# Two mixers of a transformer block: convolution taps moved to VectorE, reciprocal roots to one GpSimd power, attention operands filled to 128 rows

## The chip, the cores and the metric

The kernel runs on one core of one Trainium2 chip. The metric is the time that the device takes for one execution, in microseconds (us), and smaller is better. A core has five engines that run side by side, each with an instruction queue of its own that it works through in order: TensorE (PE in the rows; PEld is its weight load), VectorE (DVE), ScalarE (ACT), GpSimd (POOL) and SyncE (SP), which here issues the transfers.

## What is computed

Two transformer blocks, one behind the other, on 512 tokens of 1024 channels, all in float32. The first (a differential attention layer and a Fourier layer with their feed-forwards) is touched by the change only in the norm of its queries and keys. The second has two layers, each a mixer and a convolutional feed-forward. The mixer runs four branches on quarter-width groups of the projected stream and joins them:

```python
proj = h @ w_in[l]
a_in, b_q, b_k, b_v, c_in, d_cq, d_ckv, d_kr = jnp.split(proj, SPLIT_POINTS, axis=-1)
# (a) gated convolution over 31 tokens, then layer norm and silu
a = a_in[..., :GROUP_W] * jax.nn.sigmoid(a_in[..., GROUP_W:])
a = depthwise_conv(a, conv_a_w[l], conv_a_b[l])
o_a = jax.nn.silu(layer_norm(a, ln_a_g[l], ln_a_b[l]))
# (b) grouped-query attention: rms norm of q and k, rotation, softmax(q k) v, heads of 64
# (c) spatial gating: gelu, layer norm of one half, a 128x128 product over tokens, times the other half
# (d) latent attention: rms norms, two small projections, rotation, heads of 64 + 32 channels
mix = jnp.concatenate([o_a, o_b, o_c, o_d], axis=-1) @ w_out[l]
h = layer_norm(DEEPNORM_ALPHA * h + mix, ln_mix_g[l], ln_mix_b[l])
```

## The kernel before

Activations lie feature-major, 128 channels on the partitions and 512 tokens along a row. Each large product is made of three passes over operands that are split in a high and a low part (`mm3`, lines 246 to 256: L250 low weights or activations first, L252 high with high, L254 the rest). `split` makes the parts: ScalarE copies the high part (L222), VectorE or GpSimd subtracts it to get the low part (L223). Weights arrive in three raw buffers, and their split parts live in four buffers each, so a unit of weights can be split only when the products that used an older one are done.

`mixer` is written as a list of 38 steps. Ahead of them stand: the projection of branch (b) with `head_rope` for each of four token tiles (rms norm, rotation), the constants of the attention operands, the projection of branch (a) into `ap` (padded by 15 columns at both ends), then `gate` for four token tiles (branch (c): gelu on ScalarE, mean and variance on VectorE, a reciprocal root, the scaling L1022, gain and shift L1023 and L1024, a split), each followed by `top` of the first head, two products `gelu_u`, and `shift` of the first head.

A step (h, t) works on head h of eight and key tile t of four. `top` (L1118, L1119) multiplies queries by keys and takes each query's maximum on VectorE; `shift` (L1125) turns the maxima into a row of the query operand, so that the score product subtracts them; `scores` (L1132 to L1134, exponential L1136) and `values` (L1142) follow; `sums` (L1151, L1153) and `leave` (L1163) divide and write the head's output three and five steps after its last. Maxima of head h + 1 are taken in the first two steps of head h. Steps 0 to 3 also carry `latent` (branch (d)'s down projection, two reciprocal roots at once, L1003 uses them), steps 4 and 5 the rest of branch (c), and steps 7 to 18 `mla_in` and `turn_mla`, which make the operands of the four latent heads, in tiles that `mla_tiles` takes at steps 7 and 14. Step 26 ends the convolution (`last`, `conv_out`). The output product begins behind the steps and takes the convolution's two chunks sixth and seventh of eight.

The convolution has 31 taps on each of two channel chunks. `conv_steps` gives nine of them to VectorE (L1253 and L1255, one instruction each, into `ya`) and 22 to GpSimd (a product L1259 into `cx` and an addition L1261 into `yb`, two instructions each); `conv_out` adds `yb` to `ya` (L1232). Its VectorE instructions may be placed only behind the last gate's scaling (`self.mark`); its GpSimd instructions have no such limit.

A reciprocal root is `rsqrt` (L285 to L291): twelve VectorE instructions on a few values per partition, a bit trick and three rounds of refinement. `head_rope` calls it through `rstd` (20 times in the first attention, four times per mixer), `latent` and `gate` directly (four times each per mixer). The other norms use `pow_half` (L314), one GpSimd instruction.

The framework decides the order of instructions on each engine when the program is built, from the order in which they are written, their dependencies and estimated durations; `issue_after(x)` keeps what is written inside it behind x on x's engine. On the chip that order is fixed.

Of the kernel before, what the change touches and what calls it, by code (L numbers as in the profile page):

```python
# [28 lines left out]
# columns of the packed feature-major vectors  # L29
# [19 lines left out]
# columns of the packed row vectors  # L49
# [15 lines left out]
class Seg:  # L65
    """a run of tokens: columns lo..lo+w of x(k) for feature chunk k, columns off..off+w of the split activations"""
# [11 lines left out]
class Part:  # L78
    """tokens that share a PSUM bank in a product, and the segments that norms take one after the other"""
# [5 lines left out]
class Ps:  # L85
    """PSUM pool with a number of buffers per tag"""
# [8 lines left out]
class RmsMod:  # L95
    """rms norm with gain, scale and shift, into the split activations H"""
# [10 lines left out]
    def ahead(self, xn, seg, r=None):  # L107
        """normed values without gain and shift"""
        pr = self.net.row_bcast(self.sums(seg) if r is None else r)
        for k in range(KD):  # L110
            self.net.V.tensor_tensor(xn[:, k, seg.cols()], seg(k), pr, ALU.mult)
        self.early[seg.off] = xn
# [31 lines left out]
class LayerNorm:  # L144
    """layer norm of the stream in place, and its split in H (or each chunk handed to out)"""
# [27 lines left out]
class Net:  # L173
# [16 lines left out]
    def phase(self, ctx, name, tbufs, reuse="tile"):  # L190
        """open the scratch pool of a phase"""
# [22 lines left out]
    # ---- weights: raw float32 in, split into two float32r parts that add up to it  # L214
# [21 lines left out]
    def units(self, src, ks, n):  # L236
        """ks blocks of n columns, as many per unit as fit"""
# [8 lines left out]
    def mm3(self, outs, lhs, start, stop):  # L246
        """outs: list of (psum, rhs hi, rhs lo); lhs: (hi, lo)"""
# [13 lines left out]
    def later(self, steps, work):  # L261
        """have work done behind that many steps of products"""
        self.pending.append((self.steps + steps, work))

    def product(self, outs, lhs):
        """outs: list of (psum, k -> rhs hi, k -> rhs lo); lhs: list over k of (hi, lo)"""
# [4 lines left out]
    def constant(self, dst, rows, one, eng=None):  # L271
        """fill rows of a float32r tile [p, m, n] with 0 or 1"""
        (eng or self.G).memset(dst[rows].bitcast(F32), float(one))

    # ---- small vector arithmetic
    def rstd(self, dst, src, scale, eps):
# [3 lines left out]
        self.rsqrt(dst, v)  # L280

    def rsqrt(self, dst, v):
        V, w = self.V, v.shape[1]
        hv, t = self.small(w), self.small(w)
        V.tensor_scalar(t.bitcast(I32), v.bitcast(I32), 1, None, ALU.logical_shift_right)  # L285
        V.tensor_scalar(dst.bitcast(I32), t.bitcast(I32), -1, 0x5F3759DF, ALU.mult, ALU.add)
        V.tensor_scalar(hv, v, -0.5, None, ALU.mult)
        for _ in range(3):
            V.tensor_tensor(t, dst, dst, ALU.mult)  # L289
            V.tensor_tensor(t, t, hv, ALU.mult)  # L290
            V.scalar_tensor_tensor(dst, t, 1.5, dst, ALU.add, ALU.mult)  # L291

    def bcast(self, dst, cols):
        """dst psum [128, 128*n]: row vector of cols[128 tok, n] on every partition"""
# [3 lines left out]
    def col_sums(self, dst, x):  # L298
        """dst psum [128 tok, n]: sums over the partitions of x [128, n*128 tok]"""
# [11 lines left out]
    def pow_half(self, dst, v):  # L311
        """dst = v ** -0.5 on GpSimd"""
# [17 lines left out]
    def row_ln(self, acc, accq, w, n):  # L330
        """rstd and mu*rstd per token, on every partition; sums over n channels"""
# [22 lines left out]
    # ---- setup  # L354
# [39 lines left out]
    # ---- the nine modulation vectors of a layer, for one or both conditions  # L394
# [47 lines left out]
    def fill(self, n):  # L442
        """advance the pending modulation vectors by n steps"""
# [16 lines left out]
    def norm_scale(self, l, i, msc):  # L460
        """g * (1 + scale) for norm i of layer l: [128, 8, 2]"""
# [7 lines left out]
    # ---- product that ends in the stream: weights stationary, one unit list per chunk of output features.  # L469
    # The last chunks go segment by segment, so that the norm of one segment runs beside the product of the next.  # L470
# [21 lines left out]
    # ---- gated feed-forward on the split activations H  # L492
# [79 lines left out]
    # ---- first block, layer 0: differential attention  # L572
    def head_rope(self, pt, G, out, tabs):
        """pt psum [128, G*64] -> out: rms norm over 64, gain and rotation folded in the tables"""
# [18 lines left out]
    def rotate(self, src, cosg, sing, o3, q):  # L593
        """src [128, G, 4q]; pairs are (0,q), (2q,3q) blocks; sing holds -sin first, +sin second"""
# [11 lines left out]
    def rope_tables(self, cos, sin, g, w, tiles, scale=1.0):  # L606
        """cos [128, 4, w], sin signed; g [128, w]: tables with the gain folded in"""
# [21 lines left out]
    def qkv(self, H, QT, KT, VV):  # L629
        """queries and keys normed, rotated, feature-major; values token-major; context tokens are tiles 4 and 5"""  # L630
# [52 lines left out]
    def diff_attention(self, QT, KT, VV, O, keep):  # L683
        """O[h]: split feature-major outputs of head h. p0 - lam*s0/s1*p1 stands for the attention; the factor 1/s0 of
        each query goes into the norm over the head's channels: 1/s0 / sqrt(ms/s0^2 + eps) = 1/sqrt(ms + eps*s0^2)."""
# [115 lines left out]
    # ---- first block, layer 1: Fourier mix on half spectra  # L801
# [74 lines left out]
    # ---- second block  # L876
    def proj_tm(self, us, n, H, tt):
        """token-major product of token tile tt"""
# [12 lines left out]
    def mixer(self, l, H, norm):  # L891
# [19 lines left out]
        # attention operands per pair of heads: queries and keys feature-major, one head per block, then a row that  # L911
        # takes minus the maximum of each query (ones on the side of the keys); values token-major with ones between
# [6 lines left out]
        def constants(q, k, vv, rows, zero):  # L919
# [50 lines left out]
        def step(n):  # L970
            for _ in range(n):
                with self.tc.issue_after(self.mark):
                    next(conv, None)
# [543 lines left out]
```

## Time and profile before

| | us |
|---|---|
| median of 3 timed runs (3626.2 to 3633.18) | 3630.28 |
| span of the profiled execution, first to last instruction | 3633.2 |
| TensorE busy | 3425.2 (94%) |
| TensorE weight loads busy | 2839.1 (78%) |
| VectorE busy | 2084.7 (57%) |
| ScalarE busy | 1267.5 (35%) |
| GpSimd busy | 517.0 (14%) |

The profile lists no other time for its own execution than the span, and the span is as long as the longest timed run. It is one execution, recorded by the hardware. "Busy" of TensorE is the time in which at least one product is under way; products overlap, so a busy TensorE need not run at full pace. The granted clock is the share of full speed at which TensorE is allowed to run: 0.5 is 1.2 GHz and 1.0 is 2.4 GHz, and a value between them is a mean over a stretch with both. Idle time before an instruction is put down to the instruction that ended last before it could start. `x16` is a count, `128x512 f32` a shape (partitions by columns).

### The profile page before, as it was taken

Reading aid. Unit: us, or ns where it says so; the run is one execution under the profiler, and the core shown is the slowest. Engines: PE = TensorE matmul, PEld = TensorE weight load, DVE = VectorE, ACT = ScalarE, POOL = GpSimd, SP = SyncE. Lnnn points to the kernel's source line nnn. Section 1 sums busy time; section 2 is a strip of 40 time slices with the busy share of each in tenths; the row PEclk is TensorE's granted clock in tenths of the full one; section 3 lists DMA queues with packets and bytes.
Section 4 is the critical chain, followed back from the end, with each engine's and each line's share of the span. In section 5 each row is a group of like instructions: output and inputs, shape, how many; then the busy total and the mean of one; then the engine's idle time right before and its main releaser. Section 6 shows DMA issues by size and latency. Waiting matters only on the chain.

```text
span 3633.2 us, 44413 instructions
## 1 busy us (share of the span) xinstructions
PE 3425.2 (94%) x17540; PEld 2839.1 (78%) x17540; DVE 2084.7 (57%) x3447; ACT 1267.5 (35%) x2180; POOL 517.0 (14%) x481
## 2 busy tenths in 40 slices
PE   7999999999999999999999999669999994999998
PEld 5888888777787778888888888557888873688887
DVE  6554355667664555333463336985744679666556
ACT  3211214336542224222452224235533441554333
POOL 1000001015410001000120003740100049020001
PEclk9999999999999999999999999879999996899999
DMA  6343352120045563333223333101333320023232
GB/s 222 122 141 112 101 161 72 50 70 1 24 154 160 181 195 123 99 95 97 74 99 93 93 98 91 41 21 47 93 95 97 93 80 14 18 70 110 90 102 64
DMA packets 99449, 341.80 MB, mean 94 GB/s; under 512 B 10916, under 2 KB 14116, under 8 KB 98984
## 3 DMA queue, kind: packets, MB, share of 16 engines
q1 hardware_dynamic: 99240, 338.96, 30.0%
q8 instruction: 138, 2.26, 0.3%
q14 instruction: 71, 0.58, 0.1%
HBM read 336.82 MB, written 2.10 MB: 93 GB/s over the span
## 4 chain that ended last, share of the span: by engine, by line
PE 35%; issue 6%; DVE 5%; POOL 4%; ACT 1%; ACTq 0%; DVEq 0%; POOLq 0%
PE mm L250 12%; PE mm L254 11%; PE mm L252 11%; POOL yb L1261 2%; POOL cx L1259 1%; DVE wl L223 1%; DVE ya L1255 0%; DVE s L290 0%; DVE s L291 0%; DVE s L289 0%; DVE t L164 0%; DVE t L165 0%; ACT H L222 0%; POOL s L314 0%; ACT X L166 0%
## 5 line engine op out<-in xcount | busy, mean ns | idle before, releaser
L222 ACT ACTIVATE wh<-wr 128x1024 fp32r<-128x1024 f32 (+4 forms) x505 | 510.9, 1014 | 1364.3 <-PE mm L252 894.2
L250 PE MATMUL mm<-H,wh 128*128 128x512 f32 (+1 forms) x2592 | 968.0, 374 | 11.6 <-DVE nm L1119 5.8
L254 PE MATMUL mm<-H,wl 128*128 128x512 f32 (+1 forms) x2592 | 963.0, 372 | 1.5 <-DVE wl L223 1.4
L252 PE MATMUL mm<-H,wh 128*128 128x512 f32 (+1 forms) x2592 | 964.2, 372 | 0.0
L223 DVE TENSOR_TENSOR wl<-wr,wh 128x1024 fp32r<-128x1024 f32 (+4 forms) x505 | 602.5, 1194 | 445.5 <-ACT wh L222 435.7
L250 PEld LDWEIGHTS mm<-H,wh 128*128 128x128 f32 x2592 | 494.6, 191 | 103.5 <-DVE nm L1119 6.5
L254 PEld LDWEIGHTS mm<-H,wl 128*128 128x128 f32 x2592 | 493.9, 191 | 85.8 <-DVE wl L223 2.3
L252 PEld LDWEIGHTS mm<-H,wh 128*128 128x128 f32 x2592 | 495.0, 191 | 83.5 <-issue 0.5
L254 PE MATMUL mm<-ah,wl 128*128 128x512 f32 (+1 forms) x1216 | 445.9, 367 | 0.0
L252 PE MATMUL mm<-ah,wh 128*128 128x512 f32 (+1 forms) x1216 | 443.8, 365 | 0.0
L250 PE MATMUL mm<-al,wh 128*128 128x512 f32 (+1 forms) x1216 | 443.1, 365 | 0.0
L252 PEld LDWEIGHTS mm<-ah,wh 128*128 128x128 f32 x1216 | 228.3, 188 | 42.4
L250 PEld LDWEIGHTS mm<-al,wh 128*128 128x128 f32 x1216 | 228.3, 188 | 42.3 <-issue 1.2
L254 PEld LDWEIGHTS mm<-ah,wl 128*128 128x128 f32 x1216 | 228.7, 188 | 39.5
L419 DVE SCALAR_TENSOR_TENSOR macc<-wr,SC,macc 128x1024 f32<-128x1024 f32 x133 | 168.3, 1281 | 94.3 <-DMA wr<-w_mod 93.7
L568 DVE SCALAR_TENSOR_TENSOR X<-mm,ng,X 128x512 f32<-128x512 f32 (+1 forms) x120 | 81.3, 678 | 244.8 <-PE mm L254 244.7
L314 POOL TENSOR_TENSOR s<-s,mhalf 128x2 f32<-128x2 f32 (+1 forms) x26 | 21.0, 806 | 1355.5 <-ACT s L321 816.4
L250 PE MATMUL mm<-wl,H 128*128 128x512 f32 (+2 forms) x480 | 180.7, 378 | 33.7 <-DVE wl L223 30.4
L528 DVE TENSOR_TENSOR act<-act,mm 128x512 f32<-128x512 f32 x88 | 60.3, 686 | 240.0 <-PE mm L254 239.8
L254 PE MATMUL mm<-wh,H 128*128 128x512 f32 (+2 forms) x480 | 176.7, 370 | 0.3
L252 PE MATMUL mm<-wh,H 128*128 128x512 f32 (+2 forms) x480 | 176.4, 368 | 0.0
L156 POOL TENSOR_TENSOR cx<-X 128x512 f32<-128x512 f32 x5 | 9.3, 1851 | 1005.7 <-DVE X L1267 638.2
(348 smaller groups left out, 4921.9 us busy)
## 6 DMA issues: line engine op xcount, KB each, us to landing
wr<-gu SPq DMA_DIRECT2D x176, 512.0 KB, 3.5
wr<-w_mod SPq DMA_DIRECT2D x136, 512.0 KB, 4.2
wr<-up SPq DMA_DIRECT2D x88, 512.0 KB, 3.5
wr<-dn SPq DMA_DIRECT2D x48, 448.0 KB, 3.4
wr<-down SPq DMA_DIRECT2D x32, 448.0 KB, 3.3
wr<-qkv SPq DMA_DIRECT2D x24, 512.0 KB, 4.3
wr<-dn SPq DMA_DIRECT2D x24, 512.0 KB, 3.6
wr<-w_out SPq DMA_DIRECT2D x16, 512.0 KB, 3.5
```

Source lines behind the costliest of these rows:

```text
L156: (net.G if k < KD - 1 else net.V).tensor_tensor(self.acc[:, sl], self.acc[:, sl] if k > 1 else seg(0), seg(k), ALU.add)
L222: self.S.activation(hi, src, AF.Copy)
L223: (eng or self.V).tensor_tensor(lo, src, hi.bitcast(F32), ALU.subtract)
L250: self.PE.matmul(pt, lh, rl, start=start, stop=False)
L252: self.PE.matmul(pt, lh, rh, start=False, stop=False)
L254: last = self.PE.matmul(pt, ll, rh, start=False, stop=stop)
L314: G.tensor_tensor(dst, v, self.mhalf.to_broadcast([P, w]), ALU.pow)
L419: self.V.scalar_tensor_tensor(acc[c], raw, s, acc[c], ALU.mult, ALU.add)
L528: self.V.tensor_tensor(to, to, pu, ALU.mult)
L568: self.V.scalar_tensor_tensor(s(d), pt, gate[0][:, d, s.cond:s.cond + 1], s(d), ALU.mult, ALU.add)
L1259: G.tensor_tensor(x, ap[:, j, t2:t2 + T], wt(t2).to_broadcast([P, T]), ALU.mult)
L1261: G.tensor_tensor(yb[:, j], yb[:, j], x, ALU.add)
```

## The change

The change has four parts. First, `rsqrt` is gone: `rstd`, `latent` and `gate` call `pow_half`, one GpSimd instruction, instead. Second, all 31 taps are VectorE instructions into `ya`; `yb`, `cx` in the convolution and the two additions in `conv_out` are gone. The taps are handed out two (one per chunk) in each of steps 1 to 25 and four in every fourth step, behind the latest `top` on VectorE (`self.mark2`) instead of the last gate. Third, the attention operands get zeros in all rows behind their channels (64 to 127 for branch (b), 96 to 127 for branch (d), which had none) and the products take all 128 rows instead of 96 or 97. Fourth, the constants of the latent heads' tiles are filled by GpSimd instead of VectorE. Comments are removed as well. The core of the diff:

```diff
     def rstd(self, dst, src, scale, eps):
         w = src.shape[1]
         v = self.small(w)
         self.V.tensor_scalar(v, src, scale, eps, ALU.mult, ALU.add)
-        self.rsqrt(dst, v)
-
-    def rsqrt(self, dst, v):
...
+        self.pow_half(dst, v)
...
-        def constants(q, k, vv, rows, zero):
+        def constants(q, k, vv, row):
             for i in range(2):
-                for x in (k, *q) if zero else ():
-                    self.constant(x[i], rows, 0)
-            eng = G if zero else V
-            eng.memset(vv[:, :, 1], 1.0)
-            self.constant(k[0], slice(rows.start, rows.start + 1), 1, eng)
+                for x in (k, *q):
+                    self.constant(x[i], slice(row, P), 0)
+            G.memset(vv[:, :, 1], 1.0)
+            self.constant(k[0], slice(row, row + 1), 1)
...
-        constants(q, k, vv, slice(64, 96), True)
+        constants(q, k, vv, 64)
...
         def step(n):
             for _ in range(n):
-                with self.tc.issue_after(self.mark):
+                with self.tc.issue_after(self.mark2):
                     next(conv, None)
...
-            self.rsqrt(r, ss)
+            self.pow_half(r, ss)
...
-            self.rsqrt(r, mv[:, 1:2])
-            self.mark = V.tensor_scalar(t, t, mv[:, 0:1], r, ALU.subtract, ALU.mult).ins
+            self.pow_half(r, mv[:, 1:2])
+            V.tensor_scalar(t, t, mv[:, 0:1], r, ALU.subtract, ALU.mult)
...
-            constants(*mla[i], slice(96, 97), False)
+            constants(*mla[i], 96)
...
-            PE.matmul(st, d["q"][0][:96, qi * P:qi * P + P], d["k"][0][:96], start=True, stop=True)
+            PE.matmul(st, d["q"][0][:, qi * P:qi * P + P], d["k"][0], start=True, stop=True)
...
-            PE.matmul(st, kl[:96, ks], qh[:96], start=True, stop=False)
-            PE.matmul(st, kh[:K, ks], qh[:K], start=False, stop=False)
-            PE.matmul(st, kh[:96, ks], ql[:96], start=False, stop=True)
+            PE.matmul(st, kl[:, ks], qh, start=True, stop=False)
+            PE.matmul(st, kh[:, ks], qh, start=False, stop=False)
+            PE.matmul(st, kh[:, ks], ql, start=False, stop=True)
...
-                 26: [lambda: step(99), last]}
+                 26: [last]}
...
-            if i > 5:
-                step(1)
+            if 0 < i < 26:
+                step(2 if i % 4 == 3 else 1)
...
     def conv_out(self, ya, O, v):
         V, S = self.V, self.S
-        for j in range(2):
-            V.tensor_tensor(ya[:, j], ya[:, j], self.yb[:, j], ALU.add)
...
     def conv_steps(self, ap, ya, w, b):
-        """31 taps, the first on VectorE and the others on GpSimd"""
-        V, G = self.V, self.G
-        NV = 9
-        yb = self.tile([P, 2, T], "yb")
-        for t in range(max(NV, 31 - NV)):
+
+        for t in range(31):
             for j in range(2):
-                wt = lambda t: w[:, 31 * j + t:31 * j + t + 1]
+                wt = w[:, 31 * j + t:31 * j + t + 1]
                 if t == 0:
-                    V.tensor_scalar(ya[:, j], ap[:, j, :T], wt(0), b[:, j:j + 1], ALU.mult, ALU.add)
-                elif t < NV:
-                    V.scalar_tensor_tensor(ya[:, j], ap[:, j, t:t + T], wt(t), ya[:, j], ALU.mult, ALU.add)
-                t2 = NV + t
-                if t2 < 31:
-                    x = self.tile([P, T], "cx", 2) if t else yb[:, j]
-                    G.tensor_tensor(x, ap[:, j, t2:t2 + T], wt(t2).to_broadcast([P, T]), ALU.mult)
-                    if t:
-                        G.tensor_tensor(yb[:, j], yb[:, j], x, ALU.add)
+                    self.V.tensor_scalar(ya[:, j], ap[:, j, :T], wt, b[:, j:j + 1], ALU.mult, ALU.add)
+                else:
+                    self.V.scalar_tensor_tensor(ya[:, j], ap[:, j, t:t + T], wt, ya[:, j], ALU.mult, ALU.add)
             yield
-        self.yb = yb
```

## Rows read from the trace of the kernel before

**Rows 1.** The page's busy tenths in 40 equal slices of the span, two of its lines.

```profile
PE   7999999999999999999999999669999994999998
PEclk9999999999999999999999999879999996899999
```

**Rows 2.** Stretches: length, each engine's busy us (instructions), granted clock, DMA share, GB/s.

```profile
2300.00:2404.00 104.00, 48.73 (x217) 40.59 (x216) 102.37 (x125) 12.86 (x30) 103.84 (x80) 0.71 0.05 15
2404.00:2440.00 36.00, 32.27 (x137) 24.58 (x137) 25.91 (x106) 17.21 (x52) 0.00 (x0) 0.81 0.13 44
2440.00:2507.00 67.00, 66.86 (x326) 46.74 (x324) 38.97 (x91) 41.78 (x88) 1.94 (x3) 0.97 0.08 25
2990.00:3093.00 103.00, 46.08 (x212) 39.17 (x211) 101.61 (x123) 12.86 (x30) 102.57 (x79) 0.71 0.05 13
```

**Rows 3.** What TensorE waited for, 2284 to 2404: total us, times, longest us.

```profile
PE tr L983 <- ACT t L1003: 16.2, 1, 16.2
PE mm L250 <- DVE wl L223: 14.8, 2, 12.0
PE tr L296 <- DVE nm L1119: 13.8, 2, 13.2
```

**Rows 4.** VectorE by line and shape, 2300 to 2404: count, busy us, mean ns, idle.

```profile
L1255 DVE SCALAR_TENSOR_TENSOR ya<-ap,vec,ya 128x512 f32<-128x512 f32 x16 | 21.9, 1388 | 0.0
L290 DVE TENSOR_TENSOR s<-s,s 128x1 f32<-128x1 f32 x12 | 11.8, 993 | 0.2
L1022 DVE TENSOR_SCALAR t<-t,s,s 128x256 f32<-128x256 f32 x4 | 4.8, 1212 | 0.0
L1119 DVE TENSOR_REDUCE nm<-mm 128x1 f32<-128x512 f32 x7 | 4.6, 672 | 0.0
L287 DVE TENSOR_SCALAR s<-s 128x1 f32<-128x1 f32 x3 | 0.4, 137 | 0.0
```

**Rows 5.** The same view, 2405 to 2497.

```profile
L1119 DVE TENSOR_REDUCE nm<-mm 128x1 f32<-128x512 f32 x24 | 15.8, 681 | 3.7 <-PE mm L1118 3.5
L290 DVE TENSOR_TENSOR s<-s,s 128x2 f32<-128x2 f32 x7 | 1.1, 154 | 0.1
L1234 DVE TENSOR_TENSOR t<-ya 128x512 f32<-128x512 f32 x1 | 0.7, 692 | 0.0
```

**Rows 6.** TensorE by line and shape, 2300 to 2404.

```profile
L250 PE MATMUL mm<-wl,H 128*128 128x352 f32 x25 | 10.9, 436 | 14.8 <-DVE wl L223 14.8
L250 PE MATMUL mm<-H,wh 128*128 128x512 f32 x16 | 7.8, 490 | 3.0 <-DVE nm L1119 3.0
L254 PE MATMUL mm<-wh,H 128*128 128x256 f32 x21 | 5.9, 283 | 0.0
```

**Rows 7.** TensorE in order of time: start, us, what; beside a full granted clock.

```profile
2457.01 0.28 PE L254 MATMUL mm<-wh,ck 128*128 128x256 f32 x1
2457.12 0.39 PE L1132 MATMUL mm<-q,k 96*128 96x512 f32 x1
2457.36 0.39 PE L1133 MATMUL mm<-q,k 96*128 96x512 f32 x1
2457.58 0.39 PE L1134 MATMUL mm<-q,k 96*128 96x512 f32 x1
```

**Rows 8.** GpSimd by line and shape, whole span.

```profile
L1261 POOL TENSOR_TENSOR yb<-yb,cx 128x512 f32<-128x512 f32 x84 | 120.0, 1447 | 0.3
L314 POOL TENSOR_TENSOR s<-s,mhalf 128x2 f32<-128x2 f32 x24 | 18.9, 788 | 1355.3 <-ACT s L321 816.4 <-PE mm L254 538.1
L273 POOL MEMSET q<- 32x1024 f32 x8 | 7.4, 951 | 0.1
```

**Rows 9.** GpSimd in order of time, one row.

```profile
2263.05 0.95 POOL L273 MEMSET q<- 32x1024 f32 x1
```

**Rows 10.** VectorE in order of time, two rows.

```profile
2263.24 1.23 DVE L223 TENSOR_TENSOR wl<-wr,wh 128x1024 fp32r<-128x1024 f32 x1 [0.20 <-ACT wh L222]
...
2488.32 1.28 DVE L1232 TENSOR_TENSOR ya<-ya,yb 128x512 f32<-128x512 f32 x2
```

More of the change, by code (lines that the diff above doesn't have):

```diff
@@ L279, in rstd @@
         self.V.tensor_scalar(v, src, scale, eps, ALU.mult, ALU.add)
-        self.rsqrt(dst, v)
-    def rsqrt(self, dst, v):
[L283 to L291, printed above, removed]
+        self.pow_half(dst, v)
     def bcast(self, dst, cols):
@@ L1110, in head @@
             (q_, k_, v_), row = ((q[kk], k, vv), slice(64, 96)) if h < 4 else ((mla[kk - 2][0][0], *mla[kk - 2][1:]), slice(96, 97))
-            heads[h] = dict(q=[x[:, b] for x in q_], k=[x[:, b] for x in k_], row=row, K=row.stop,
+            heads[h] = dict(q=[x[:, b] for x in q_], k=[x[:, b] for x in k_], row=row,
                             v=v_.rearrange("p t c d -> p t (c d)")[:, :, 64 * b:64 * b + P],
@@ L1128, in scores @@
             d = heads[h]
-            K, ks = d["K"], slice(t * P, t * P + P)
+            ks = slice(t * P, t * P + P)
             st = self.bank("mm")
             (qh, ql), (kh, kl) = d["q"], d["k"]
-            PE.matmul(st, kl[:96, ks], qh[:96], start=True, stop=False)
-            PE.matmul(st, kh[:K, ks], qh[:K], start=False, stop=False)
-            PE.matmul(st, kh[:96, ks], ql[:96], start=False, stop=True)
+            PE.matmul(st, kl[:, ks], qh, start=True, stop=False)
+            PE.matmul(st, kh[:, ks], qh, start=False, stop=False)
+            PE.matmul(st, kh[:, ks], ql, start=False, stop=True)
             d["p", t] = ring()
```

## The prediction

> **What bounds the kernel now.** I began with the page's 40 slices, to see where TensorE is not full. Its busy tenths are 9 nearly everywhere except at both ends and in slices 26, 27 and 34, and there the granted clock falls too [rows 1]. At 90.8 us a slice those are 2270 to 2452 and 2997 to 3088: the two mixers. The stretches show who is full instead: from 2300 to 2404 us VectorE is busy for 102.37 of 104 us and GpSimd for 103.84, TensorE for 48.73 at a mean granted clock of 0.71; the second mixer repeats this from 2990 to 3093 [rows 2]. As soon as GpSimd falls silent, at 2404, TensorE is busy for 99 of the next 103 us [rows 2]. So I cut each mixer into a stall part A (104 us) and a steps part B (36 + 67 = 103 us).
>
> The waits say which chain stalls A: TensorE's three longest waits, 16.2, 14.8 and 13.8 us, end on VectorE or on ScalarE work that VectorE fed (L1003 takes the reciprocal roots) [rows 3]. What VectorE does there is the next view. A reciprocal root is twelve tiny instructions, and those with two tensor inputs in SBUF take 0.99 us for 128x1 values [rows 4]; the same line on 128x2 values takes 0.154 us when GpSimd is silent [rows 5]. The convolution's taps (128x512) take 1.39 us [rows 4], against 0.69 for an addition of that size with GpSimd silent [rows 5]. The maximum L1119 reads PSUM and is unmoved, 0.672 against 0.681, and L287, one SBUF input and tiny, stays at 0.137 [rows 4, 5]. So GpSimd's stream of two-input instructions (1.447 us each for L1261 [rows 8]) makes VectorE wait out most of one of them per two-input instruction.
>
> The Trainium skill has this in "SBUF — State Buffer", section "Who interferes with whom": a VectorE instruction with two SBUF inputs contends with a GpSimd instruction that reads SBUF, and the later one waits for all of the earlier. The rows just named agree.
>
> **The change part by part, A.** VectorE's 102.4 us in A hold twelve groups of root instructions (L285 to L291, two widths) from 11.8 us (L290) down to 0.4 us (L287), together 49.8 us, and 18 taps at 1.39, 25.0 us [rows 2, 4]. The change removes the roots altogether (one instruction each on GpSimd) and lets the taps begin only behind the maxima of the next head, so about six of 62 remain here: 6 x 0.64 = 3.8 us. That leaves at most 102.4 - 49.8 - 25.0 + 3.8 = 31.4 us, and less because the rest loses its waits too (L1022 takes 1.21 us for 256 columns [rows 4], where 512 take 0.69 with GpSimd silent [rows 5]). TensorE's own work in A at full clock: 75 products of 352 columns, 48 of 512 and 61 of 256 (three lines of each shape [rows 6]) and 33 others of the 217 [rows 2]. Rows at full clock start 0.11 us apart after 256 columns and 0.23 after 512 [rows 7], so 0.16 for 352 by columns: 75 x 0.16 + 48 x 0.23 + 61 x 0.11 + 33 x 0.24 = 37.7 us. TensorE becomes the bound of A.
>
> What stalls remain? The root is now a round trip to GpSimd: 0.79 us for the power itself [rows 8], at eight roots in the gate and latent steps 6.3 us, if nothing covered them. Products of the next token tile cover most; VectorE's own queue (a gate's scaling stands behind its root, and the splits and maxima behind that) is the cover that can fail. I add 6 us for that, and 8 us for restarts at the lower clock and the fourth weight unit of the latent projection, which needs a buffer that the products just before it free. A comes to 52 us, with bounds 40 (nearly no stall) and 70 (two waits left that are as long as today's longest, 37.7 + 2 x 16.2). It gains 52 us, bounds 64 and 34.
>
> **B.** Here the taps come to rest. A tap's price with GpSimd silent is in no row; its nearest are the two additions of 128x512 back to back, 1.28 us, 0.64 each [rows 10], and the single one, 0.69 [rows 5]. I take 0.64, since taps follow one another: 62 x 0.64 = 39.7 us (42.9 at the other end), of which 3.8 lie in A. VectorE is busy for 25.91 + 38.97 = 64.9 us in B [rows 2]. It loses the latent roots left there (three groups like L290's 1.1 us [rows 5] and small ones, 4 us), two row fills that go to GpSimd (2 us) and the two additions of yb (1.3 us). So 64.9 - 7.3 + 39.7 - 3.8 = 93.5 us in 103: VectorE goes from 63% to 91%, level with TensorE's 99. Behind a tap in its queue stand the next maxima, whose banks TensorE's next products need, and the splits of queries and keys; but a tap is 0.64 us and a step of this part takes about 4 (103 us for some 25 steps), so the cover is the spare banks. On the other side A's latent and gate work no longer drags into B's first 36 us, where the clock is 0.81 [rows 2]. I take B at 105 us, 2 longer; bounds 94 (VectorE's work alone) and 124 (six groups of four steps with ten taps, 6.4 us, each, half of it exposed: 19 more).
>
> A rule speaks against this edit: the Trainium skill's "Perfetto Trace Analysis", section "Optimizing Scalar/DVE Operations", holds that with VectorE saturated, giving work to ScalarE or even GpSimd may pay, with the warning that the two share a port. By the first half, B pays for the taps in full (my first rival below); by the warning, A's gain is real. Rows 4 against rows 5 side with the warning.
>
> **Zero fill.** Each pair of heads of the latent attention adds four fills of 32x1024 to GpSimd, 0.95 us each [rows 8], and the ones: about 5 us per pair, at steps 7 and 14. What waits behind them in GpSimd's queue is only the convolution's norm at step 26. The head that needs them begins five steps later, about 20 us. Do they hold taps up? One row says no: a 128x1024 split took 1.23 us right beside a fill [rows 9, 10], twice a 0.64 us addition at twice the size. So 0, and up to 5 us per pair in the range if they did. The products grow from 96 or 97 to 128 rows: a 96-row product follows a 128-row one after 0.11 us and the next follow 0.24 and 0.22 later [rows 7], the pace of 128 rows. So 0.
>
> **Elsewhere.** The norms of query and key heads (20 in the first attention, four at each mixer's start) swap twelve tiny VectorE instructions for one power. TensorE is full there [rows 1], and the transposes that need the result come one tile late, which hides the round trip; if that cover failed, 28 x 0.79 = 22 us. I count -4 to +4, and take -3.
>
> **The sum.** Per mixer -52 + 2 = -50; two mixers -100; elsewhere -3: -103 us. The profiled span is 3633.2 us, at the top of the timed runs and 2.9 above their median of 3630.3. So 3530 for a profile like this one, 3527 for a median.
>
> **The rivals.**
> 1. VectorE becomes the bound of B. For it: 91% on an engine whose queue is in order, beside a TensorE that waits for its maxima. Against it: in A it did keep 98% busy [rows 2], so 93.5 us can fit. Price: B at its upper bound, 21 us longer than now, and A at 55: 2 x (-49 + 21) - 3 = -59, some 3571.
> 2. Slower than before: the taps in front of the maxima let TensorE fall idle at every head, and its clock falls to 1.2 GHz for the steps. TensorE's work in B is about 92 us at 2.4 GHz (99 busy, less half of the 13.7 us that 0.81 over 36 us means at the lower level), 184 at 1.2. It decides when B exceeds 155 us, a mean granted clock under 0.6. At 184: 2 x (81 - 52) - 3 = +55, 3685. Against it: the only stretch near that clock is A, 0.71, where TensorE is idle more than half the time [rows 2].
> 3. The change doesn't free the taps: their 1.39 us isn't GpSimd's doing. Then B's VectorE work is 56 x 1.39 + 57.6 = 135 us, 32 longer, and only the roots' removal remains: 2 x (-52 + 32) - 3 = -43, 3587. Against it: lines that read at most one SBUF tensor kept their price in A [rows 4, 5].
> 4. Better: TensorE runs A at its own pace and B without the slow clock: 2 x (-64 - 7) - 3 = -145, some 3485.
>
> **How the numbers follow.** My forecast has 0.70, rival 1 0.14, rival 4 0.09, rival 3 0.04, rival 2 0.03. The range 3480 to 3585 holds the forecast with its bounds, rivals 1 and 4. Faster by over 0.2% (7 us, about what a measurement of this kernel can tell from no change): 0.95; within: 0.02; slower: 0.03, rival 2.
>
> **What will show it.** Right: GpSimd nearly idle in the mixers, no VectorE instruction on 128x1 values near 1 us; a tap at 0.60 to 0.70; stall part near 52 us with TensorE over 70% busy; VectorE 85 to 95% busy in the steps; the 128-row products at 0.23 us. Wrong: a tap near 1.4 us (rival 3); TensorE waiting for maxima or splits in B for over 20 us (rival 1), with the clock under 0.7 (rival 2); a GpSimd power waiting behind a fill; the convolution's norm late, so that the output product waits for its chunks.

## The result, and the profile after

The changed kernel takes 3484.7 us (median of 4 runs, 3482.4 to 3490.2) against 3631.7 for the kernel before on the same chip: 0.9595 of the time, 95% interval 0.9582 to 0.9608. Timed once more beside other kernels it was 0.9603 (0.9589 to 0.9617). The profiled span is 3488.4 us against 3633.2, 144.8 us less. The forecast was 3527 with 3480 to 3585: the direction held, the range held, and the time came out 42 us below the forecast, at that of rival 4 (3485).

The page of the changed kernel, busy tenths in 40 slices; it answers [rows 1]:

```profile
PE   7999999999999999999999999999999999999998
...
DVE  6554444565746455433355333678655567865556
...
POOL 1000000225510000100021000320100022120001
PEclk9999999999999999999999999999999999999999
```

The holes of the two mixers are gone from TensorE's row and from the clock's. The stretches answer [rows 2]; the same columns (length, busy us and instructions of PE, PEld, DVE, ACT, POOL, granted clock, DMA share, GB/s):

```profile
2300.00:2334.00 34.00, 34.00 (x190) 30.16 (x190) 20.90 (x56) 14.73 (x38) 4.54 (x6) 1.00 0.14 39
2334.00:2370.00 36.00, 34.12 (x165) 25.95 (x163) 32.51 (x90) 18.18 (x51) 5.27 (x6) 0.86 0.12 45
2370.00:2437.00 67.00, 63.95 (x290) 43.52 (x289) 56.85 (x113) 37.75 (x78) 6.30 (x9) 0.95 0.05 16
```

What was 104 us of stalls at a clock of 0.71 is 34 us of a TensorE that never stops, at full clock. The two stretches behind it are as long as I had cut the steps before, 103 us; VectorE is busy for 89.4 of them. (How long the steps really take, the landmarks below measure.) TensorE's waits, 2300 to 2470, answer [rows 3]; totals of 16.2, 14.8 and 13.8 us have become:

```profile
PE mm L285 <- DVE nm L1107: 1.5, 1, 1.5
PE mm L1106 <- DVE nm L1107: 1.5, 1, 1.5
PE mm L1106 <- ACT k L222: 1.2, 1, 1.2
```

VectorE by line and shape, 2300 to 2437 (count, busy us, mean ns, idle before), answers [rows 4, 5]; L1238 is the tap, L1010 the gate's scaling behind its power:

```profile
L1238 DVE SCALAR_TENSOR_TENSOR ya<-ap,vec,ya 128x512 f32<-128x512 f32 x60 | 43.5, 784 | 0.2
L1107 DVE TENSOR_REDUCE nm<-mm 128x1 f32<-128x512 f32 x30 | 19.7, 680 | 1.2 <-PE mm L1106 0.9
L1078 DVE COPY t<-KR 128x64 f32<-128x64 f32 x8 | 3.7, 464 | 0.0
L1010 DVE TENSOR_SCALAR t<-t,s,s 128x256 f32<-128x256 f32 x3 | 1.2, 415 | 1.8 <-POOL s L303 1.8
```

The tap's mean holds single ones at 0.74; six in a row took 4.03 us, 0.67 each. The scaling fell from 1.212 us to 0.415, and the whole round trips of three gates' powers left VectorE idle for 1.8 us. Products of 128 rows follow one another 0.23 us apart, as those of 96 did in [rows 7]:

```profile
2419.84 0.39 PE L1121 MATMUL mm<-q,k 128*128 128x512 f32 x1
2420.07 0.39 PE L1122 MATMUL mm<-q,k 128*128 128x512 f32 x1
2420.30 0.40 PE L1120 MATMUL mm<-q,k 128*128 128x512 f32 x1
```

GpSimd by line and shape, 2290 to 2437, answers [rows 8]:

```profile
L273 POOL MEMSET q<- 32x1024 f32 x4 | 3.7, 948 | 3.0 <-ACT cq L222 3.0
...
L303 POOL TENSOR_TENSOR s<-s,mhalf 128x2 f32<-128x2 f32 x4 | 3.5, 870 | 27.3 <-DVE s L987 27.3
L303 POOL TENSOR_TENSOR s<-s,mhalf 128x1 f32<-128x1 f32 x4 | 2.7, 675 | 25.0 <-DVE s L1008 25.0
```

To set the kernels against one another I cut each mixer at four events that all have: the first maximum of the first head, the first maximum of the third head, the last maxima, and GpSimd's first sum of the output norm (line 156). In the changed kernel's first mixer these are, in order of time:

```profile
2295.93 0.68 DVE L1107 TENSOR_REDUCE nm<-mm 128x1 f32<-128x512 f32 x1
...
2337.67 0.69 DVE L1107 TENSOR_REDUCE nm<-mm 128x1 f32<-128x512 f32 x1
...
2422.49 1.27 DVE L1107 TENSOR_REDUCE nm<-mm 128x1 f32<-128x512 f32 x2
...
2451.55 1.29 POOL L156 TENSOR_TENSOR cx<-X 128x512 f32<-128x512 f32 x1 [18.74 <-DVE X L1212]
```

They give 41.8 us (gates and latent projections), 84.8 (the other heads) and 29.1 (tail). The same for all kernels, first mixer / second mixer, in us:

| kernel (its trace) | gates, latent | other heads | tail | both mixers | time / before [95%] |
|---|---|---|---|---|---|
| before | 111.7 / 111.5 | 76.1 / 76.0 | 34.4 / 34.3 | 444.0 | 1 |
| changed | 41.8 / 41.8 | 84.8 / 80.7 | 29.1 / 29.1 | 307.2 | 0.9595 [.9582, .9608] |
| changed, again | 41.7 / 41.8 | 78.8 / 78.7 | 29.1 / 29.1 | 299.3 | 0.9603 [.9589, .9617] |
| taps alone | 43.3 / 42.9 | 89.6 / 86.5 | 32.5 / 32.5 | 327.5 | 0.9682 [.9669, .9695] |
| roots alone | 113.6 / 113.6 | 66.4 / 66.4 | 32.7 / 34.3 | 427.0 | 0.9935 [.9922, .9949] |
| fill and 128 rows alone | 111.8 / 111.0 | 71.8 / 75.0 | 32.7 / 32.7 | 434.9 | 0.9977 [.9968, .9986] |
| changed, no fill | 41.8 / 41.8 | 87.4 / 88.0 | 34.0 / 35.4 | 328.4 | 0.9666 [.9653, .9679] |
| that, constants on GpSimd | 41.8 / 41.8 | 82.8 / 83.4 | 34.0 / 34.0 | 317.8 | 0.9624 [.9603, .9644] |
| that, late transposes | 41.8 / 41.8 | 79.1 / 78.6 | 29.1 / 29.0 | 299.5 | 0.9594 [.9577, .9612] |
| changed + old stream | 108.4 / 108.3 | 80.7 / 81.2 | 29.1 / 30.7 | 438.4 | 0.9969 [.9956, .9982] |
| changed + fills | 55.1 / 47.4 | 86.7 / 80.9 | 29.1 / 29.1 | 328.3 | 0.9685 [.9668, .9703] |
| changed, half the taps | 41.7 / 41.7 | 71.5 / 71.6 | 32.7 / 32.6 | 291.8 | 0.9568 [.9552, .9583] |
| changed, taps earlier | 41.8 / 41.8 | 74.9 / 74.8 | 29.1 / 29.1 | 291.6 | 0.9564 [.9547, .9581] |

The last maxima are no clean cut in TensorE's order: in the kernel before, roots alone, fill alone and half the taps, 337 to 343 products start between the second and the third landmark and 154 behind it, in the others 342 to 356 and 141. Between these two groups only the sum of "other heads" and "tail" compares. Of the span's 144.8 us the mixers hold 444.0 - 307.2 = 136.8; 4.8 lie between them (468.0 us before, 463.3 after, from the first norm's sum to the second mixer's first maximum). Two traces of the changed kernel differ by 8 us in the mixers, so for differences below that the last column decides.

### The profile page after: what moved, and what is told of

It is laid out like the page before. It is cut to its first block, busy times and chain, and to the rows that moved or that the text cites. A ratio compares the mean times of both kernels' runs of the same rounds, so it can differ in the third digit from the quotient of the medians.

```text
span 3488.4 us, 43926 instructions
## 1 busy us (share of the span) xinstructions
PE 3393.3 (97%) x17540; PEld 2818.9 (81%) x17540; DVE 1939.2 (56%) x2995; ACT 1266.1 (36%) x2180; POOL 367.1 (11%) x377
## 4 chain that ended last, share of the span: by engine, by line
PE 42%; DVE 4%; ACT 2%; POOL 1%; issue 1%; DVEq 0%; ACTq 0%; POOLq 0%
PE mm L250 13%; PE mm L254 13%; PE mm L252 12%; PE tr L1130 1%; DVE ya L1238 1%; DVE wl L223 0%; PE tr L285 0%; ACT H L222 0%; PE mm L1120 0%; DVE nm L1107 0%; PE mm L1139 0%; PE tr L290 0%; ACT X L166 0%; DVE t L164 0%; PE mm L1122 0%
## 5 line engine op out<-in xcount | busy, mean ns | idle before, releaser
L303 POOL TENSOR_TENSOR s<-s,mhalf 128x2 f32<-128x2 f32 (+4 forms) x70 | 78.0, 1114 | 1586.4 <-ACT s L310 817.3
L222 ACT ACTIVATE ah<-act 128x512 fp32r<-128x512 f32 (+1 forms) x132 | 88.0, 667 | 163.0 <-DVE act L545 109.9
```

What stands on the lines that cost most here:

```text
L222: self.S.activation(hi, src, AF.Copy)
L303: G.tensor_tensor(dst, v, self.mhalf.to_broadcast([P, w]), ALU.pow)
```

## The experiments

My theory was that GpSimd's two-input stream made VectorE's two-input instructions long, and that this was the stall part. The first three runs do one part of the change each, on the kernel before.

**Taps alone.** All taps on VectorE behind the maxima, no stream; roots, fills and rows as before.

```diff
-                    G.tensor_tensor(x, ap[:, j, t2:t2 + T], wt(t2).to_broadcast([P, T]), ALU.mult)
...
-                        G.tensor_tensor(yb[:, j], yb[:, j], x, ALU.add)
...
+                    self.V.scalar_tensor_tensor(ya[:, j], ap[:, j, t:t + T], wt, ya[:, j], ALU.mult, ALU.add)
...
-                with self.tc.issue_after(self.mark):
+                with self.tc.issue_after(self.mark2):
```

> The kernel before with the convolution's edit alone: all 62 taps on VectorE behind the maxima, no stream of products and additions on GpSimd; the roots stay twelve tiny VectorE instructions, and the fills and the 96 rows stay. My theory (the GpSimd stream made the tiny two-input instructions of the roots long): with GpSimd silent a root costs 12 x some 0.1 to 0.15, about 1.5 us, in place of 8 or more, so nearly all of the gain is here already. The changed kernel is 146 us faster than before; I expect 115 to 140 of them here, 3492 to 3517 us, with the line that took 993 ns on 128x1 at 0.15 us in the gates. Rival (the number of tiny instructions is what stalls TensorE, and only taking them away helps): a root stays long, and the gain is under 60 us, 3570 or more.

Measured: 3518.7 us against 3635.1, 116.5 less (0.9682), at the lower end of what I expected. VectorE by line and shape, 2300 to 2335, in this run:

```profile
L291 DVE SCALAR_TENSOR_TENSOR s<-s,s 128x1 f32<-128x1 f32 x12 | 1.8, 155 | 0.2
L290 DVE TENSOR_TENSOR s<-s,s 128x1 f32<-128x1 f32 x12 | 1.8, 155 | 0.2
...
L1022 DVE TENSOR_SCALAR t<-t,s,s 128x256 f32<-128x256 f32 x4 | 1.6, 409 | 0.0
```

The very instructions that took 993 ns in [rows 4] take 155 here, at the same place, and with them L1022 falls from 1212 to 409. The gates and latent part is 43.3 us, almost the changed kernel's 41.8, with all twelve instructions of every root still there. The number of VectorE's instructions stalled nobody; the stream did, and the rival falls. How much of the stall the long roots made, and how much the long taps, scalings and splits beside them, this run does not take apart.

**Roots alone.** One GpSimd power for each root, the stream stays.

```diff
-        self.rsqrt(dst, v)
+        self.pow_half(dst, v)
```

(the same for the latent and the gate's root)

> The kernel before with the roots' edit alone: one GpSimd power for each root, with the convolution's stream still on GpSimd. My theory: VectorE loses its tiny waiting instructions, but the powers now share GpSimd's queue with instructions of 1.45 us, the taps left on VectorE stay at 1.39 us, and the stream of 104 us now runs on beside the steps; so part of the gain, 50 to 100 us, 3530 to 3580. Rival (roots alone did it): 130 us or more, 3500 or less. Rival (powers behind the stream stall the gates as much as the old roots): under 30 us, 3600 or more.

Measured: 3611.0, 24 us less (0.9935): half of the least that I expected, and what the second rival said. The stall part is not shorter at all, 113.6 us. From 2300 to 2404, VectorE's tap and its scaling, and GpSimd's power:

```profile
L1255 DVE SCALAR_TENSOR_TENSOR ya<-ap,vec,ya 128x512 f32<-128x512 f32 x16 | 28.4, 1812 | 0.0
...
L1022 DVE TENSOR_SCALAR t<-t,s,s 128x256 f32<-128x256 f32 x4 | 4.7, 1184 | 19.3 <-POOL s L314 19.3
```

```profile
L314 POOL TENSOR_TENSOR s<-s,mhalf 128x1 f32<-128x1 f32 x4 | 2.2, 552 | 0.0
```

A power takes 0.55 us, but VectorE idles 19.3 us for four of them: they stand in GpSimd's queue behind the stream. VectorE lost 38 us of work in that part (64.3 busy of 104 against 102.4) and TensorE gained nothing. What this run gains lies behind it: 10 us a mixer in the other heads, and 461.0 us in place of 468.0 between the mixers, where the head norms stand.

**Fill and 128 rows alone.** The constants of the latent tiles go to GpSimd with it.

```diff
-            constants(*mla[i], slice(96, 97), False)
+            constants(*mla[i], 96)
...
-            PE.matmul(st, kl[:96, ks], qh[:96], start=True, stop=False)
+            PE.matmul(st, kl[:, ks], qh, start=True, stop=False)
```

> The kernel before with the zero fill and the 128-row products alone. My prediction has this edit at 0 us, with up to 5 us per pair of heads if the fills held others up: 3630 to 3650, near 3632. The fills stand in GpSimd's queue among the stream here, so if anything it is slower. Rival (128 rows cost or gain something in the products): over 10 us either way.

Measured: 3626.7, 8 us less (0.9977). I had said 0 or slower. Which part of the edit gained it, this run does not show; the next ones take the same edit apart in the changed kernel.

**The changed kernel without the fill** (the last diff undone on the changed kernel).

> The changed kernel without the zero fill: products of 96 and 97 rows, and the few constants of a pair written by VectorE, as before the change. In the changed kernel's trace the fills of the second pair stood beside a copy of 128x64 that took 2.50 us in place of 0.17 and taps at 0.96, and TensorE then waited 1.50 us. If that is a hold of VectorE by the fills and it reaches the end: 1 to 6 us faster than the changed kernel, 3479 to 3484. If the spare time of VectorE covers it: no difference, 3484 to 3486.

Measured: 3513.2 (0.9666), 23 to 26 us slower than the changed kernel by the ratios, where I expected a small gain. VectorE and TensorE where the operands of the third pair of heads are made and the fourth head's maxima are taken, in this run, in order of time:

```profile
2359.87 0.91 DVE L273 MEMSET k<- 1x1024 f32 x1 [0.25 <-issue]
...
2362.03 2.07 DVE L1239 SCALAR_TENSOR_TENSOR ya<-ap,vec,ya 128x512 f32<-128x512 f32 x3
2364.01 1.28 DVE L1108 TENSOR_REDUCE nm<-mm 128x1 f32<-128x512 f32 x2
```

```profile
2362.16 0.64 PE L1088 MATMUL tr<-ident,t 128*96 128x128 f32 x4 [0.87 <-DVE t L593]
...
2364.75 0.51 PE L1107 MATMUL mm<-k,q 96*128 96x512 f32 x1 [1.71 <-DVE nm L1108]
```

Without the zero fill the row of ones is written by VectorE again: 0.91 us in its queue, just ahead of the rotation that TensorE's transposes wait for. TensorE idles 2.58 us here, and in the changed kernel 1.48. Two runs take this apart.

**Products of 96 rows, constants on GpSimd.**

```diff
-            eng = G if zero else V
+            eng = G
```

> As the run without the zero fill (3513 us, products of 96 and 97 rows), but the few constants of a pair, one row of 1x1024 and the ones, written by GpSimd and not by VectorE. In that run's trace the row's fill took VectorE 0.91 us just ahead of the first products of the second pair, and TensorE then idled 2.58 us in place of 1.48, with its granted clock at 0.50 for longer. If that place made the 25 us: back to 3482 to 3492. Rival (the 96-row products cost them): stays at 3508 to 3518.

Measured: 3498.5 (0.9624), 15 us (by the ratio, with some 9 either way) better than the run before it, though not the changed kernel's time. What was left stood in the tail, 34.0 us against 29.1; TensorE there:

```profile
2439.27 1.19 PE L285 MATMUL tr<-ident,s 128*128 128x128 f32 x8 [1.52 <-POOL s L303]
```

In the order that the framework wrote for TensorE, and that both traces show, the transposes of the convolution's norm stand two products and a group of sums earlier than in the changed kernel, and TensorE waits for the power. Of the 5 us more, 1.5 are this wait; behind it the granted clock falls, to a mean of 0.90 over the tail, against 1.00 in the changed kernel. The traced execution took 3507.8 us, 9 above the median, so the table's row for this kernel is rather long.

**The same with the transposes moved.**

```diff
+            with self.tc.issue_after(self.lastmm):
+                self.conv_out2(ya, O, v)
```

(conv_out2 is the second half of conv_out, from the transposes on; lastmm is the last product of the scores)

> As the run with 96-row products and the constants of a pair on GpSimd (0.9624 of the time before, 10 us behind the changed kernel), with the transposes of the convolution's norm moved behind the last score product. In that run TensorE's written order had them two products and a sum earlier than in the changed kernel; it waited 1.5 us for the power there and ran the next 8 us at a granted clock of 0.5 to 0.8, and the time from the last maximum to the first sum of the output norm was 34.0 us a mixer against 29.1. If the order alone makes these 5 us a mixer: 29 to 30 us there, and 0.959 to 0.961 of the time before. If the 96-row products or the missing fills cost them: 34 us again and 0.962 to 0.963.

Measured: 0.9594, the tail 29.1 and 29.0 us: the changed kernel's time, with 96-row products and no zero fill. So the fill and the 128 rows are worth nothing that this can tell, as forecast; what the edit brought is that VectorE writes no row and that the written order came out better.

**The old stream beside the changed kernel.**

```diff
+                G.tensor_tensor(x, ap[:, j, 9 + t:9 + t + T], wt.to_broadcast([P, T]), ALU.mult)
...
+                    G.tensor_tensor(yb[:, j], yb[:, j], x, ALU.add)
```

(22 times for both halves; in the trace it runs from the convolution's input on, through the gates, as before the change; the sum is not used)

> The changed kernel with the old GpSimd stream beside it, its results unused: 22 taps per half as product and addition of 128x512, two inputs each, from the gates on. VectorE still does all 62 taps, so no work is taken from it. My theory (two-input instructions of both engines hold each other up): a tap goes from 0.66 to about 1.4 us and VectorE's other two-input instructions follow; the stream's 86 instructions at 1.3 to 1.45 us cover some 115 us of each mixer, and the powers stand in its queue. Most of the gain goes: 3580 to 3660 us. Rival (what counted was the number of VectorE's instructions): VectorE does the same as in the changed kernel, so under 3510.

Measured: 3622.3 (0.9969): the gain is gone, as expected, but by a way that I had not expected. VectorE, then GpSimd, in order of time:

```profile
2381.37 0.19 DVE L587 TENSOR_TENSOR KR<-mm,rm 128x32 f32<-128x32 f32 x1 [24.76 <-ACT t L992]
...
2381.64 12.63 DVE L1240 TENSOR_SCALAR ya<-ap,vec 128x512 f32<-128x512 f32 x1
```

```profile
2379.92 0.70 POOL L303 TENSOR_TENSOR s<-s,mhalf 128x2 f32<-128x2 f32 x1
```

A latent root stood behind the stream in GpSimd's queue, and VectorE idled 24.76 us for ScalarE's work on it; then the first tap of the second half, which has a single tensor input, was held 12.63 us until the stream's next gap, at 2394. The second mixer has the same two rows, 24.76 and 12.63 us. Almost no two-input tap ran beside the stream, so this run shows that the stream alone undoes the change, not that it does so by the taps' price. That price beside a stream is in [rows 4] and in the run with roots alone.

**A stream that only writes.** Six fills of 128x1024 in place of two products and two additions (`G.memset(yb, 0.0)`).

> The changed kernel with a GpSimd stream that only writes: 22 times six fills of 128x1024 per mixer, some 0.95 us each by the fills in its trace, 125 us in all. It keeps GpSimd as busy as the old stream but reads nothing. If only GpSimd's reading holds VectorE up, as the Trainium skill has it (SBUF - State Buffer, section Who interferes with whom), taps stay at 0.66 and only the powers pay, queued behind a fill: 3490 to 3530 us. In the changed kernel's trace, though, taps took 0.96 beside fills and a copy of 128x64 took 2.50 in place of 0.17; by that row the copies and one-input instructions are held and taps half so: 3530 to 3570. Rival (any busy GpSimd does it): as the two-input stream, 3580 or more.

Measured: 3523.5 (0.9685), inside the first range. VectorE by line and shape, 2300 to 2440, GpSimd filling for 106.6 us of it:

```profile
L1242 DVE SCALAR_TENSOR_TENSOR ya<-ap,vec,ya 128x512 f32<-128x512 f32 x56 | 41.0, 798 | 0.2
...
L1079 DVE COPY t<-KR 128x64 f32<-128x64 f32 x8 | 6.2, 776 | 0.0
L1011 DVE TENSOR_SCALAR t<-t,s,s 128x256 f32<-128x256 f32 x4 | 4.0, 1008 | 8.5 <-POOL s L303 8.4
...
L1013 DVE TENSOR_TENSOR t<-t,p 128x256 f32<-128x256 f32 x4 | 1.7, 420 | 0.1
```

The two-input instructions keep their price (798 against 784 in the changed kernel, 420 against 423), and the other heads take what they took. The copy and the scaling, with one tensor input each, do not: 776 against 464 (170 in single rows without a fill beside them) and 1008 against 415. So the second reading was right about the copies and wrong about the taps. The 13 and 6 us more in the gates are mainly powers queued behind fills (8.4 us of idle in the first mixer) and held scalings. Another 9 us against the changed kernel's second trace lie ahead of the second mixer's first maximum (470.6 against 461.7 between the mixers), where the fills run already beside the head norms. The Trainium skill ("SBUF — State Buffer", section "Who interferes with whom") has both halves: an instruction with two SBUF inputs contends with a GpSimd instruction that reads SBUF and not with one that only writes, while copies and `tensor_scalar` can run in a mode that contends with GpSimd's instructions at large. The expectation cites only the first half, which holds for the taps alone. These rows agree with both; the mode in which an instruction ran is in no row.

**Half the taps.** Every second tap left out, 32 of 62; the convolution is not the whole one here.

> The changed kernel with every second tap left out (32 of 62 taps a mixer, so the convolution is not the reference's); all else stands where it stood. It asks what bounds the steps. VectorE loses 30 x 0.66 = 20 us a mixer. If VectorE bounds the steps (the first rival of my prediction), both mixers shrink by most of that: 30 to 40 us, 3445 to 3455. If TensorE bounds them, only its few waits for maxima behind taps go, with the slow clock behind them: the gain of the run with the taps spread otherwise, 8 to 16 us, 3468 to 3477. If taps cost nothing at all: 3482 to 3487.

Measured: 3474.3 (0.9568). Both mixers together are 7.5 us shorter than in the changed kernel's second trace, though VectorE lost 20 us of work in each. The last 67 us of the steps, here and then in that trace:

```profile
2370.00:2437.00 67.00, 66.33 (x319) 46.45 (x319) 49.61 (x97) 41.08 (x79) 6.83 (x9) 1.00 0.10 32
```

```profile
2375.00:2442.00 67.00, 63.27 (x303) 43.09 (x302) 59.81 (x114) 39.98 (x80) 6.30 (x9) 1.00 0.09 30
```

TensorE is busy for 66.33 of 67 us with half the taps and for 63.27 with all of them: TensorE bounds the steps, but for a few us of waits, and the first rival falls.

**The taps earlier.** 12 of the 31 pairs in the gates' and latent part; the first added line stands behind each of the two gelu_u.

```diff
+            step(2)
...
-            if 0 < i < 26:
-                step(2 if i % 4 == 3 else 1)
+            if i < 26:
+                step(2 if i < 4 else 0 if i in (8, 10, 15) else 1)
```

> The changed kernel with the taps spread otherwise: 12 of 31 pairs lie in the part of the gates and latent projections, where VectorE was busy for 20.90 of 34 us, none at steps 8, 10 and 15, and no double ones at the heads' ends. In the changed kernel's trace two maxima stood behind three taps (2.06 us), TensorE waited 1.48 us for them, and its granted clock was 0.50 or little more for the next 13 us, in each mixer. If the taps' places made that wait: the clock stays, 4 to 8 us per mixer, 3468 to 3478. Rival (taps ahead of the latent roots stall the first part, or the wait has another cause): 3483 or more.

Measured: 3476.4 (0.9564), and for certainty once more beside the changed kernel itself:

> The taps spread otherwise once more, on the chip on which the changed kernel runs too. By the first timings it is 0.9564 (0.9547 to 0.9581) of the time before against 0.9595, and its two mixers together are 15.6 us shorter in the trace. If that is its gain, 8 to 16 us below the changed kernel here; if chips made the difference, 0 to 4.

> The changed kernel itself once more, beside the others on one chip: 0.9582 to 0.9608 of the time before, by its first timing. It is the base for the run with the taps spread otherwise.

Measured on one chip: 3473.8 (0.9567, 0.9547 to 0.9587) against 3487.3 (0.9603, 0.9589 to 0.9617): 13 us better than the changed kernel, with all taps, and equal to the kernel with half of them. The other heads fell from 78.7 to 74.8 us. The expectation put the gain down to the clock behind the wait, and that is not what these two traces show: over the other heads the mean granted clock was 1.00 in the changed kernel and 0.98 here. What fell is TensorE's idle time, from 6.2 of 78.8 us to 1.6 of 74.8. It is the best version here. Its stretches of gates and latent projections and of the last 67 us of the steps:

```profile
2300.00:2334.00 34.00, 34.00 (x204) 30.74 (x204) 30.05 (x72) 13.68 (x32) 4.13 (x6) 1.00 0.13 38
...
2370.00:2437.00 67.00, 66.35 (x315) 45.83 (x315) 55.00 (x109) 41.94 (x85) 6.31 (x9) 0.98 0.09 28
```

In the first VectorE is busy 30.05 of 34 us, against 20.90, and TensorE does not notice.

## Why the prediction was right, and where it missed

**What bounds the kernel: right.** GpSimd's stream made VectorE's instructions long, and VectorE's queue stalled TensorE. Taps alone show it: 993 ns became 155, and the stall was gone with all roots still there. That it was the roots in that queue more than the taps is argued from their 49.8 us, not shown. Two readings on the way were wrong. The 16.2, 14.8 and 13.8 us of [rows 3] are totals, the last two of two waits each, and the longest single waits were 16.2, 13.2 and 12.0. And against rival 3 I held that instructions with at most one SBUF tensor had kept their price: L1022 has one, and it fell from 1212 to 409 ns when the stream was gone. Rival 3 falls all the same, by the tap itself, 0.66 to 0.67 us in a row.

**Stall part, 104 to 52 us: the term that was mis-sized.** By the page's stretches it became 34, by the landmarks 111.7 became 41.8: a gain of 70 us a mixer where I had 52. The sum was 37.7 of TensorE's work, 6 for round trips of powers and 8 for restarts and the fourth weight unit. TensorE's work came out at 34.0 us, busy for all of the stretch, 4 under the forecast; of the 14 us of stalls none came. Powers of 128x1 took 0.55 and once 1.06 us, not 0.79, but that is not it: products of the next token tile covered every one of them, as the text says they might, and with no idle time there was no slower clock to restart from. I charged the cover's failure and its consequence as if both were likely. This is 2 x 18 of the 42 us missed. Rival 4, with TensorE at its own pace here, was the right picture of this part (64 of the 70 us). Its other half, steps 7 us shorter without any slow clock, was not: in the second trace of the changed kernel the clock never fell in the steps, and they were 2.6 us shorter; in the first they were 3.4 us longer in the first mixer and 0.7 shorter in the second. That its time was met to the microsecond is luck.

**Steps, 103 to 105 us: right.** Other heads and tail together took 110.5 us before, and 113.9 and 109.8 after, 107.9 in the second trace, where the forecast was 2 us more than before. VectorE's work there came out at 89.4 of 103 us (forecast 93.5), the tap at 0.66 to 0.67 in a row (forecast 0.64, other end 0.69). TensorE waited for maxima for 2 to 4 us a mixer, far from the 20 of rival 1, and half the taps gained no more than better places did.

**Zero fill, 0: right in the product, wrong in the company it keeps.** The 128-row products and the fills are worth nothing that can be told (late transposes run). But the same edit moves a row's fill off VectorE. I counted that as 2 us of VectorE's load in the steps; it was a place in its queue just ahead of what TensorE waits for, worth some 15 us over both mixers, with 9 either way. Another 11 or so (0.9624 to 0.9594, with 10 either way) came from an order that only the framework's estimates had changed, which no reading of the old trace could have given. My "fills don't hold taps" is nearly right: beside the changed kernel's fills four taps took 3.85 us, 0.96 each, behind a copy that was held 2.50.

**Elsewhere, -3: right in sign, small in size.** The runs with roots on GpSimd have 461 to 463 us between the mixers (but for the one whose fills begin at the head norms, 470.6), the runs with the old roots 468.0 to 469.5: about -7, at the head norms of the second mixer. Nothing that can be told came in the first attention.

**The parts do not add in the order in which I added them.** Alone, taps gain 116.5, roots 24, fill 8; that these add up to 149, near the whole change's 147, is chance. On top of the taps the roots bring 0.9682 to 0.9666, within the intervals, since a root of twelve quiet instructions is cheap too, and the fill on top of both brings 23 to 26. I had put the 49.8 us of root instructions down as removed work; removing the stream shrank the slow ones to about a sixth.

## What to carry to other kernels

When tiny instructions take a microsecond, ask which other engine streams beside them before you take them away: here the same instructions were cheap as soon as the stream was gone, and moving them behind that stream in the other queue gained next to nothing. A busy share says little about where an engine's work may stand: 24 taps a mixer, some 16 us, cost nothing beside the gates (41.8 us with 24 taps there and with 8), and 0.9 us in front of the wrong transposes cost several. Where a part of a sum is a cover that can fail, price it once as the end of the range and not inside the likeliest value.

## What the runs showed of the hardware

The same wait did not always cost the same. In both traces of the changed kernel TensorE waits 1.48 us for two maxima that stand behind three taps. First trace, then second, each in stretches of 5 us from the one with the wait on:

```profile
2355.00:2360.00 5.00, 3.42 (x19) 2.47 (x17) 5.00 (x14) 1.61 (x6) 0.00 (x0) 0.97 0.00 0
2360.00:2365.00 5.00, 4.70 (x18) 3.70 (x17) 5.00 (x15) 2.67 (x8) 0.00 (x0) 0.50 0.02 5
2365.00:2370.00 5.00, 5.00 (x16) 3.48 (x16) 3.26 (x7) 1.08 (x3) 0.00 (x0) 0.50 0.00 0
```

```profile
2360.00:2365.00 5.00, 3.42 (x20) 2.47 (x19) 5.00 (x14) 1.43 (x6) 0.00 (x0) 1.00 0.00 0
2365.00:2370.00 5.00, 4.09 (x27) 3.11 (x25) 5.00 (x17) 3.70 (x12) 0.00 (x0) 1.00 0.02 5
2370.00:2375.00 5.00, 5.00 (x25) 3.41 (x25) 5.00 (x14) 2.75 (x8) 0.00 (x0) 1.00 0.00 0
```

In the first the granted clock falls to 0.50, which is 1.2 GHz, and this mixer's other heads take 84.8 us; in the second it stays at 1.00, 2.4 GHz, and they take 78.8. (In the first trace's second mixer the clock stood at 0.50 for some 7 us, not for the 13 that the expectation of the earlier taps has for each mixer, and the other heads take 80.7. Behind a later wait of 1.50 us the first trace dips once more in its first mixer, to 0.89 and 0.77 in two stretches; the second trace never does.) One kernel, nearly the same waits, 6 us apart: the waits of a trace can be compared between kernels, the clock behind a short one only over several runs.

A GpSimd stream without gaps can hold a VectorE instruction far longer than one of its own instructions lasts: 12.63 us for a tap of one tensor input (0.54 in the changed kernel), beside instructions of 1.0 to 1.3 us, in both mixers of the run with the old stream.
